# Where the modulation sums are accumulated, and where relu's squares stand before they are split

## The chip, the cores and the metric

The kernel runs on one core of one Trainium2 chip. The metric is device time in microseconds (us); before the change it is 3557.34 us, the median of 3 runs (3553.0 to 3562.2).

## What is computed

Two transformer blocks run one after the other on 512 tokens of 1024 features, all in fp32. The first block has two layers (a sparse and a stick-breaking attention side by side, then a feed-forward part). The second has two layers as well (latent attention, then a gated linear attention); it also sees 256 context tokens, and its norms are scaled and shifted by a modulation that is computed from one vector `c`, and for the context from `c_ctx`. Cut to what the change touches:

```python
# both blocks, each layer
ff = jnp.square(jax.nn.relu(hf @ w_ff1)) @ w_ff2        # [512, 1024] @ [1024, 4096], then back

# second block, each of two layers; ada_w[i] is [1024, 6144]
m_lat = (silu_c  @ ada_w[i] + ada_b[i]).reshape(B, N_MOD, 1, D)
m_ctx = (silu_cc @ ada_w[i] + ada_b[i]).reshape(N_MOD, D)
```

## The kernel before

TensorE (PE) does the large products on float32r operands. Every fp32 operand is kept as two float32r parts: `split` (lines 163 to 167) lets ScalarE (ACT) cast x to the high part and VectorE (DVE) subtract it from x for the low part; `wload` (169 to 195) does the same for a block of a weight with ACT and GpSimd (POOL, L194, two operations a block). `mac3` (208 to 213) then issues three products for one (L211, L212, L213). `feat_major` makes one tile, 128 features by up to 512 tokens, in one PSUM bank.

PSUM's eight banks are three pools: `mm` with two, `s` with four, `tp` with two. A tile's buffer is reused when the last instruction that reads it has ended. Weights in raw form have three buffers (`wraw`), their parts two each.

**The feed-forward part** (`mlp`, from line 619) goes through 8 chunks of 512 hidden features. `first(c + 1)` computes the 4 tiles of the next chunk, each of 24 products, in the two `mm` banks in turn (in chunk 0 in `mm` and `s` by turns, with 256 tokens at a time); then `second(c)` multiplies the chunk before with the second weight, 8 tiles of 12 products, in `mm` and `s` by turns. After each of the first product's tiles `square_parts` (517 to 530) takes relu's square from the bank and leaves its two parts in SBUF tiles `hid`: L522 on VectorE takes max(ps, 0) * r into an SBUF tile `t` (r is the norm's factor; in the second block there is none, and ACT takes the relu), L525 on ACT squares `t` into the high part of `hid`, L529 on VectorE squares `t` in place (in chunk 0 ACT does it, L527), and L530 subtracts.

**The modulation** (`ada`, from line 1334) is a vector times a matrix, made on VectorE as a background of the first block's two feed-forward parts: layer 0's modulation beside the first, layer 1's beside the second. For each of 12 groups u of 512 columns there are accumulators `aacc`, [128, 512] in SBUF, two of them (for `c` and for `c_ctx`; layer 1 needs the second only for the first four groups). Four steps q each load 512 KB of the matrix (`araw`, two buffers, one load ahead) and add two row blocks to each accumulator:

```python
nc.vector.scalar_tensor_tensor(a, raw[:, k], sc, a, op0=ALU.mult, op1=ALU.add)     # L1372
```

The first of a group writes without adding (L1370). Then `total` (1345 to 1355) splits each accumulator (L165 on ACT, L166 on VectorE, into SBUF tiles `t`), lets PE sum over the partitions with a column of ones, once for each part (L1351, L1352, into a `tp` bank), copies the row that results and sends it to DRAM. `total` of a group is called at the beginning of the next. When all groups are there, the sums are read back and transposed into the tiles `mod`.

**What sets the order.** `mlp` steps the background twice ahead of each weight block of the first product and three times (`BG`) ahead of `second`. The program is a stream of instructions in one order, and the tile framework's scheduler sorts it into the queues of the engines; each engine then works through its queue in order, and a product, or a VectorE operation, that has to wait holds up all that stands behind it on that engine. Loads are issued by SyncE (SP), in their own queue. The fp32 sums of the norms (`total` of line 276, L280) use plain fp32 operands and the ones tile `ones`; the sums of `ada` use `onesr`, its float32r form.

## Time and profile before

| | before |
|---|---|
| median of 3 runs | 3557.34 us |
| span of the profiled execution | 3557.3 us |
| busy: PE, DVE, ACT, POOL | 93%, 64%, 43%, 33% of the span |
| feed-forward parts of the first block | about 505 to 905 and 1445 to 1850 us |
| of the second block | about 2300 to 2770 (two streams) and 3200 to 3525 us |

The profiled execution is as long as the median run, so its microseconds can be set against the runs one to one. Instruction rows give the start in us, the duration, the engine, the line of the kernel and the tile written <- the tiles read; a wait in brackets is the engine's idle time ahead of it with what released it. PEclk is the clock that TensorE was granted, as a share of full speed.

### The profile page before, as it was taken

To read this page: it belongs to the slowest core of one execution; us is meant where nothing else is said; L and a number is where in the kernel's file an instruction comes from. 1 tells how busy PE (TensorE), PEld (TensorE's weight loads), DVE (VectorE), ACT (ScalarE), POOL (GpSimd) and SP (SyncE) were. 2 spreads that over 40 slices of the span, in tenths; PEclk is the share of its full clock that TensorE was granted. 3 is DMA by queue.
4 is the path that set the end of the run, shared out by engine and by line. 5 is a ranking of instruction groups with operands and counts; after the bars stand their busy time and mean duration, and the time that the engine had idled before them with its cause. 6 is when DMAs were issued, how large, how long until landed. Compare 5 with 4: busy or idle time off the path is not lost.

```text
span 3557.3 us, 49004 instructions
## 1 busy us (share of the span) xinstructions
PE 3299.7 (93%) x18723; PEld 2843.9 (80%) x18723; DVE 2263.8 (64%) x4044; ACT 1516.0 (43%) x3323; POOL 1191.2 (33%) x688
## 2 busy tenths in 40 slices
PE   8899988988989998989999999999999899889998
PEld 8788776766878887767778888888888788878887
DVE  6755668887686567886657763723433866873445
ACT  5455543222454454432235654531221456654223
POOL 3333334333333324334431332132232222124443
PEclk8999999999999999999999999999999999999999
DMA  5212444444232235345321113122122212123332
GB/s 171 66 60 75 166 140 152 135 145 131 82 92 72 74 114 177 116 158 176 119 74 59 37 60 97 48 63 68 60 64 63 69 53 66 63 70 95 95 95 77
DMA packets 262097, 337.68 MB, mean 95 GB/s; under 512 B 17107, under 2 KB 178110, under 8 KB 261734
## 3 DMA queue, kind: packets, MB, share of 16 engines
q1 hardware_dynamic: 261862, 334.55, 29.9%
q8 instruction: 147, 2.41, 0.3%
q14 instruction: 88, 0.72, 0.1%
HBM read 305.98 MB, written 28.52 MB: 94 GB/s over the span
## 4 chain that ended last, share of the span: by engine, by line
PE 62%; DVE 22%; ACT 8%; issue 5%; DMA 2%; POOL 1%; SPq 0%; DVEq 0%; ACTq 0%; POOLq 0%
PE mm L211 13%; PE mm L213 13%; PE mm L212 13%; PE s L212 4%; PE s L211 4%; PE s L213 4%; DVE aacc L1372 3%; ACT wh L190 2%; PE s L280 2%; DMA araw<-in_ada_w_dram 2%; DVE t L166 1%; PE tp L1065 1%; DVE t L529 1%; DVE wl L194 1%; PE mm L238 1%
## 5 line engine op out<-in xcount | busy, mean ns | idle before, releaser
L194 POOL TENSOR_TENSOR wl<-wraw,wh 128x1024 fp32r<-128x1024 f32 (+2 forms) x424 | 1008.4, 2397 | 1848.4 <-ACT wh L190 1800.2
L211 PE MATMUL mm<-h,wh 128*128 128x512 f32 (+1 forms) x1916 | 728.4, 380 | 30.1 <-ACT h L1264 8.5
L213 PE MATMUL mm<-h,wh 128*128 128x512 f32 (+1 forms) x1916 | 713.6, 373 | 6.0 <-DVE h L333 3.0
L212 PE MATMUL mm<-h,wl 128*128 128x512 f32 (+1 forms) x1916 | 716.4, 374 | 2.0 <-POOL wl L194 1.6
L190 ACT CAST wh<-wraw 128x1024 fp32r<-128x1024 f32 (+3 forms) x454 | 428.4, 967 | 512.1 <-issue 328.7
L211 PEld LDWEIGHTS mm<-h,wh 128*128 128x128 f32 x1916 | 370.2, 193 | 93.1 <-ACT h L1264 10.3
L213 PEld LDWEIGHTS mm<-h,wh 128*128 128x128 f32 x1916 | 369.1, 193 | 71.6 <-DVE h L1265 4.8
L212 PEld LDWEIGHTS mm<-h,wl 128*128 128x128 f32 x1916 | 371.0, 194 | 54.8 <-POOL wl L194 2.4
L529 DVE TENSOR_TENSOR t<-t 128x512 f32<-128x512 f32 (+1 forms) x140 | 169.2, 1208 | 256.3 <-ACT hid L525 256.0
L1372 DVE SCALAR_TENSOR_TENSOR aacc<-araw,sc,aacc 128x512 f32<-128x512 f32 x280 | 295.3, 1079 | 43.8 <-DMA araw<-in_ada_w_dram 41.8
L211 PE MATMUL mm<-hid,wh 128*128 128x512 f32 (+1 forms) x848 | 294.2, 347 | 9.7 <-DVE y L541 9.7
L212 PE MATMUL mm<-hid,wl 128*128 128x512 f32 (+1 forms) x848 | 292.4, 345 | 0.0
L213 PE MATMUL mm<-hid,wh 128*128 128x512 f32 (+1 forms) x848 | 291.3, 344 | 0.0
L541 DVE TENSOR_TENSOR y<-y,mm 128x512 f32<-128x512 f32 (+1 forms) x192 | 105.4, 549 | 201.7 <-PE mm L213 201.5
L211 PE MATMUL s<-hid,wh 128*128 128x512 f32 (+1 forms) x560 | 211.5, 378 | 0.0
L213 PE MATMUL s<-hid,wh 128*128 128x512 f32 (+1 forms) x560 | 211.4, 377 | 0.0
L212 PE MATMUL s<-hid,wl 128*128 128x512 f32 (+1 forms) x560 | 211.2, 377 | 0.0
L530 DVE TENSOR_TENSOR hid<-t,hid 128x512 fp32r<-128x512 f32 (+1 forms) x176 | 180.5, 1029 | 29.8 <-ACT t L527 25.4
L525 ACT ACTIVATE hid<-t 128x512 fp32r<-128x512 f32 (+1 forms) x176 | 97.2, 554 | 231.3 <-DVE t L522 155.6
L211 PEld LDWEIGHTS mm<-hid,wh 128*128 128x128 f32 x848 | 160.7, 190 | 33.0 <-DVE y L541 6.8
L213 PEld LDWEIGHTS mm<-hid,wh 128*128 128x128 f32 x848 | 160.7, 190 | 21.2
L212 PEld LDWEIGHTS mm<-hid,wl 128*128 128x128 f32 x848 | 160.7, 190 | 21.1 <-issue 0.3
(682 smaller groups left out, 7438.1 us busy)
## 6 DMA issues: line engine op xcount, KB each, us to landing
wraw<-in_w_ff_dram SPq DMA_DIRECT2D x128, 512.0 KB
wraw<-in_mlp_w_dram SPq DMA_DIRECT2D x128, 512.0 KB
araw<-in_ada_w_dram SPq DMA_DIRECT2D x96, 512.0 KB
wraw<-in_w_in_dram SPq DMA_DIRECT2D x68, 512.0 KB
raw<-in_cmp_w_dram SPq DMA_DIRECT2D x16, 512.0 KB
td<-t SPq DMA_DIRECT2D x32, 256.0 KB
h<-td SPq DMA_DIRECT2D x32, 256.0 KB
wraw<-in_w_out_dram SPq DMA_DIRECT2D x16, 512.0 KB
```

Of the source, the lines that this page charges most:

```text
L166: self.nc.vector.tensor_tensor(l, x, h.bitcast(F32), op=ALU.subtract)
L190: i = nc.scalar.copy(h[:, x:z], raw[:, x - a:z - a]).ins
L194: e.tensor_tensor(l[:, x:z], raw[:, x - a:z - a], h[:, x:z].bitcast(F32), op=ALU.subtract)
L211: nc.tensor.matmul(ps, wh, mh, start=first, stop=False)
L212: nc.tensor.matmul(ps, wl, mh, start=False, stop=False)
L213: nc.tensor.matmul(ps, wh, ml, start=False, stop=last)
L280: self.nc.tensor.matmul(ps, self.ones, acc, start=first, stop=last)
L525: nc.scalar.activation(h, a, AF.Square)
L529: nc.vector.tensor_tensor(a, a, a, op=ALU.mult)
L530: nc.vector.tensor_tensor(lo, a, h.bitcast(F32), op=ALU.subtract)
L541: nc.vector.tensor_tensor(y, y, ps, op=ALU.add)
L1372: nc.vector.scalar_tensor_tensor(a, raw[:, k], sc, a, op0=ALU.mult, op1=ALU.add)
```

## The change

In `ada`, the accumulators are no longer SBUF tiles but the two banks of `tp`. A new `part` splits them when the group's last step is issued, into SBUF tiles `ada0` and `ada1` of float32r; where layer 1 has two accumulators, ACT only copies them to fp32 tiles instead. `total` then has the ones-products and the row's copy alone, with its result in a bank of `s`. It is called after the third step of the next group, half a group later than before, and for copies in fp32 it is one product with `ones` instead of two with `onesr`. One more step is put ahead of the last `total`.

In `square_parts`, where one stream runs alone (the two feed-forward parts of the first block and the last one of the second), the square goes back into the bank that the product came from: with r ACT squares `t` into the bank, without r VectorE multiplies max(ps, 0) with ACT's relu into it. `split` then makes the two parts from the bank. The stage with two streams keeps what it had. In `load_ctx` the transposes of the context go to `s` instead of `tp`. Comments are dropped, too; the changed kernel's lines stand up to 20 lower in the file from `square_parts` on (L1370, L1372 are L1387, L1389 there; L1351 and L1352 are L1371).

```diff
-    def square_parts(self, ps, r, h, lo, quick):
+    def square_parts(self, ps, r, h, lo, bank, quick):
...
-        nc.scalar.activation(h, a, AF.Square)
-        if quick:
-            nc.scalar.activation(a, a, AF.Square)
+        if not bank:
+            nc.scalar.activation(h, a, AF.Square)
+            if quick:
+                nc.scalar.activation(a, a, AF.Square)
+            else:
+                nc.vector.tensor_tensor(a, a, a, op=ALU.mult)
+            nc.vector.tensor_tensor(lo, a, h.bitcast(F32), op=ALU.subtract)
+            return
+        if r is not None:
+            nc.scalar.activation(ps, a, AF.Square)
         else:
-            nc.vector.tensor_tensor(a, a, a, op=ALU.mult)
-        nc.vector.tensor_tensor(lo, a, h.bitcast(F32), op=ALU.subtract)
+            nc.vector.scalar_tensor_tensor(ps, ps, 0.0, a, op0=ALU.max, op1=ALU.mult)
+        self.split(ps, h, lo)
...
-            self.square_parts(ps, None if S.r is None else S.r[:, sl], h[:, sl], lo[:, sl], c == 0)
+            self.square_parts(ps, None if S.r is None else S.r[:, sl], h[:, sl], lo[:, sl], len(streams) == 1,
+                              c == 0)
...
-        def total(u, acc):
-            for s, a in enumerate(acc):
-                h = self.t(self.tmp, [P, 512], F32R, tag="t")
-                lo = self.t(self.tmp, [P, 512], F32R, tag="t")
-                self.split(a, h, lo)
-                ps = self.ps(pool=self.tp, tag="tp")
-                nc.tensor.matmul(ps[0:1], self.onesr[:, 0:1], h, start=True, stop=False)
-                nc.tensor.matmul(ps[0:1], self.onesr[:, 0:1], lo, start=False, stop=True)
+        def part(acc):
+
+            nb = 2 if l == 0 else 1
+            if l and len(acc) == 2:
+                out = [[self.t(pool, [P, 512], F32, tag=f"ada{q}", bufs=nb)] for q in range(2)]
+                for a, (c,) in zip(acc, out):
+                    nc.scalar.copy(c, a)
+                return out
+            out = [[self.t(pool, [P, 512], F32R, tag=f"ada{q}", bufs=nb) for q in range(2)] for _ in acc]
+            for a, hl in zip(acc, out):
+                self.split(a, *hl)
+            return out
+
+        def total(u, parts):
+            for s, ms in enumerate(parts):
+                ps = self.ps(pool=self.sp, tag="s")
+                one = (self.ones if len(ms) == 1 else self.onesr)[:, 0:1]
+                for q, m in enumerate(ms):
+                    nc.tensor.matmul(ps[0:1], one, m, start=q == 0, stop=q == len(ms) - 1)
...
-            if done:
-                total(*done)
-            acc = [self.t(pool, [P, 512], F32, tag="aacc", bufs=2) for _ in range(1 if l == 1 and u >= 4 else 2)]
+            acc = [self.ps(pool=self.tp, tag="tp") for _ in range(1 if l == 1 and u >= 4 else 2)]
...
+                if q == 2 and done:
+                    total(*done)
                 yield
-            done = u, acc
+            done = u, part(acc)
+        yield
         total(*done)
...
-                ps = self.ps(pool=self.tp, tag="tp")
+                ps = self.ps(pool=self.sp, tag="s")
```

**What moves.** PE, the sum of an early group in the first feed-forward part: of before, where a tile of the first product (`mm`, from the norm's parts `h` and the weight's parts `wh`, `wl`) has the two ones-products between its own.

```order
L213 MATMUL mm_6005<-h_4549,wh_5995 128x512
L211 MATMUL mm_6005<-h_4578,wh_5995 128x512
L212 MATMUL mm_6005<-h_4578,wl_5996 128x512
L213 MATMUL mm_6005<-h_4579,wh_5995 128x512
L1351 MATMUL tp_5981<-t_5977,onesr_642 1x512
L211 MATMUL mm_6005<-h_4608,wh_5995 128x512
L212 MATMUL mm_6005<-h_4608,wl_5996 128x512
L1352 MATMUL tp_5981<-t_5978,onesr_642 1x512
L213 MATMUL mm_6005<-h_4609,wh_5995 128x512
L211 MATMUL mm_6005<-h_4638,wh_5995 128x512
```

The changed kernel, where the sum of that group stands, between two tiles:

```order
L212 MATMUL mm_6023<-h_4740,wl_5984 128x512
L213 MATMUL mm_6023<-h_4741,wh_5983 128x512
L1371 MATMUL s_6065<-ada_1120_5967,onesr_642 1x512
L1371 MATMUL s_6065<-ada_1121_5968,onesr_642 1x512
L1371 MATMUL s_6071<-ada_1122_5969,onesr_642 1x512
L1371 MATMUL s_6071<-ada_1123_5970,onesr_642 1x512
L211 MATMUL mm_6087<-h_4548,wh_6077 128x512
L212 MATMUL mm_6087<-h_4548,wl_6078 128x512
L213 MATMUL mm_6087<-h_4549,wh_6077 128x512
```

The ones-products now come in one piece, four for the two accumulators, behind the last product of a tile and ahead of the next tile's first; before, the products of one accumulator stood apart, with two products of a tile between them.

VectorE, the square of a tile of the first product in the same part, and the sum's steps around it; of before:

```order
L522 SCALAR_TENSOR_TENSOR t_6508<-mm_6483,r_94 128x512
L1372 SCALAR_TENSOR_TENSOR aacc_6429<-araw_6437,sc_718,aacc_6429 128x512
L1372 SCALAR_TENSOR_TENSOR aacc_6430<-araw_6437,sc_718,aacc_6430 128x512
L1372 SCALAR_TENSOR_TENSOR aacc_6429<-araw_6513,sc_718,aacc_6429 128x512
L529 TENSOR_TENSOR t_6508<-t_6508 128x512
L1372 SCALAR_TENSOR_TENSOR aacc_6429<-araw_6513,sc_718,aacc_6429 128x512
L530 TENSOR_TENSOR hid_1185_6326<-t_6508,hid_1184_6325 128x512
L1372 SCALAR_TENSOR_TENSOR aacc_6430<-araw_6513,sc_718,aacc_6430 128x512
L166 TENSOR_TENSOR t_6526<-aacc_6429,t_6525 128x512
```

The changed kernel, at a tile of the same chunk (`mm_6379` and `mm_6441` are two tiles' banks, `tp_6417` and `tp_6418` the accumulators):

```order
L522 SCALAR_TENSOR_TENSOR t_6404<-mm_6379,r_94 128x512
L1389 SCALAR_TENSOR_TENSOR tp_6417<-araw_6425,sc_718,tp_6417 128x512
L1389 SCALAR_TENSOR_TENSOR tp_6418<-araw_6425,sc_718,tp_6418 128x512
L1389 SCALAR_TENSOR_TENSOR tp_6417<-araw_6501,sc_718,tp_6417 128x512
L166 TENSOR_TENSOR hid_1177_6310<-mm_6379,hid_1176_6309 128x512
L1389 SCALAR_TENSOR_TENSOR tp_6417<-araw_6501,sc_718,tp_6417 128x512
L1389 SCALAR_TENSOR_TENSOR tp_6418<-araw_6501,sc_718,tp_6418 128x512
L522 SCALAR_TENSOR_TENSOR t_6466<-mm_6441,r_94 128x512
L1389 SCALAR_TENSOR_TENSOR tp_6418<-araw_6501,sc_718,tp_6418 128x512
L166 TENSOR_TENSOR hid_1179_6312<-mm_6441,hid_1178_6311 128x512
```

The square's first step L522 is followed by the subtraction L166 that reads the same bank, with one to three steps of the sum between them, the last of which needs the next load (`araw_6501` behind `araw_6425`) at the first tile. L529 and L530, which work on SBUF tiles, are gone, and L166 reads the bank.

VectorE, the beginning of the feed-forward part, where the norm of the first tokens is closed (L260 and what follows); of before:

```order
L1372 SCALAR_TENSOR_TENSOR aacc_5209<-araw_5236,sc_718,aacc_5209 128x512
L1372 SCALAR_TENSOR_TENSOR aacc_5208<-araw_5236,sc_718,aacc_5208 128x512
L1372 SCALAR_TENSOR_TENSOR aacc_5209<-araw_5236,sc_718,aacc_5209 128x512
L299 TENSOR_TENSOR acc_95<-acc_95,t_4944 128x256
L299 TENSOR_TENSOR acc_95<-acc_95,t_4973 128x256
L299 TENSOR_TENSOR acc_95<-acc_95,t_5002 128x256
L299 TENSOR_TENSOR acc_95<-acc_95,t_5031 128x256
L260 TENSOR_SCALAR acc_95<-s_5093 128x256
L194 TENSOR_TENSOR wl_5223<-wraw_5224,wh_5222 128x512
```

The changed kernel:

```order
L299 TENSOR_TENSOR acc_95<-acc_95,t_5031 128x256
L1389 SCALAR_TENSOR_TENSOR tp_5604<-araw_5605,sc_718,tp_5604 128x512
L1389 SCALAR_TENSOR_TENSOR tp_5603<-araw_5611,sc_718,tp_5603 128x512
L1389 SCALAR_TENSOR_TENSOR tp_5604<-araw_5611,sc_718,tp_5604 128x512
L1389 SCALAR_TENSOR_TENSOR tp_5603<-araw_5611,sc_718,tp_5603 128x512
L1389 SCALAR_TENSOR_TENSOR tp_5604<-araw_5611,sc_718,tp_5604 128x512
L1389 SCALAR_TENSOR_TENSOR tp_5603<-araw_5687,sc_718,tp_5603 128x512
L1389 SCALAR_TENSOR_TENSOR tp_5604<-araw_5687,sc_718,tp_5604 128x512
L260 TENSOR_SCALAR acc_95<-s_5093 128x256
L1389 SCALAR_TENSOR_TENSOR tp_5603<-araw_5687,sc_718,tp_5603 128x512
L287 TENSOR_TENSOR ry_5098<-ry_5092 128x256
```

Between the last addition to `acc` (L299) and L260 stand now seven steps of the sum's second group (`tp_5603`, `tp_5604`), four of them from the load `araw_5611` and two from `araw_5687`; before there were none, and the last step ahead of them belonged to the first group (`aacc_5209`).

## Rows read from the trace of the kernel before

**Rows 1.** Page: busy time by engine; group of lines L190 (busy, mean ns).
```profile
PE 3299.7 (93%) x18723; PEld 2843.9 (80%) x18723; DVE 2263.8 (64%) x4044; ACT 1516.0 (43%) x3323; POOL 1191.2 (33%) x688
...
L190 ACT CAST wh<-wraw 128x1024 fp32r<-128x1024 f32 (+3 forms) x454 | 428.4, 967 | 512.1 <-issue 328.7
```

**Rows 2.** Windows: us; busy PE, PEld, DVE, ACT, POOL (instructions); PEclk, DMA share, GB/s.
```profile
505.00:905.00 400.00, 352.78 (x1540) 278.61 (x1541) 329.29 (x397) 118.57 (x181) 145.84 (x56) 0.95 0.42 131
1445.00:1850.00 405.00, 366.65 (x1625) 292.55 (x1624) 277.59 (x320) 116.93 (x175) 154.28 (x60) 0.96 0.43 136
3200.00:3525.00 325.00, 324.05 (x1465) 266.26 (x1463) 129.99 (x120) 101.73 (x142) 149.64 (x60) 1.00 0.30 93
```

**Rows 3.** Waits of PE, 505 to 905 us: total us, times, longest us.
```profile
PE tp L1352 <- DVE t L166: 38.7, 13, 6.3
PE tp L1351 <- ACT t L165: 5.5, 4, 3.6
```

**Rows 4.** Waits of PE, 1445 to 1850 us.
```profile
PE tp L1352 <- DVE t L166: 27.4, 11, 3.6
PE mm L211 <- DVE t L522: 5.0, 2, 2.5
PE tp L1351 <- ACT t L165: 4.8, 3, 3.2
```

**Rows 5.** Timeline of PE at 588 us: start, duration, instruction, idle before.
```profile
587.81 0.40 PE L212 MATMUL mm<-h,wl 128*128 128x512 f32 x1
594.51 0.58 PE L1352 MATMUL tp<-t,onesr 128*1 128x512 f32 x1 [6.30 <-DVE t L166]
```

**Rows 6.** Timeline of VectorE at the same place.
```profile
588.21 3.50 DVE L1372 SCALAR_TENSOR_TENSOR aacc<-araw,sc,aacc 128x512 f32<-128x512 f32 x2 [2.44 <-DMA araw<-in_ada_w_dram]
591.63 2.82 DVE L166 TENSOR_TENSOR t<-aacc,t 128x512 fp32r<-128x512 f32 x1
```

**Rows 7.** Timeline of GpSimd at the same place.
```profile
588.30 5.60 POOL L194 TENSOR_TENSOR wl<-wraw,wh 128x1024 fp32r<-128x1024 f32 x2 [6.49 <-ACT wh L190]
```

**Rows 8.** Lines L1372 and L522: ns min/median/max, first and last start.
```profile
L1372 DVE SCALAR_TENSOR_TENSOR aacc<-araw,sc,aacc x280: 736/747/2907, 456.0 to 1740.8; 128x512 f32<-128x512 f32 x140
...
L522 DVE SCALAR_TENSOR_TENSOR t<-mm,r x64: 409/684/693, 512.9 to 1810.6; 128x512 f32<-128x512 f32 x56, 128x256 f32<-128x256 f32 x8
```

**Rows 9.** Groups of VectorE, 505 to 905 us: count, busy us, mean ns, idle before.
```profile
L1372 DVE SCALAR_TENSOR_TENSOR aacc<-araw,sc,aacc 128x512 f32<-128x512 f32 x154 | 161.8, 1077 | 13.9 <-DMA araw<-in_ada_w_dram 13.1
L166 DVE TENSOR_TENSOR t<-aacc,t 128x512 fp32r<-128x512 f32 x24 | 33.7, 1404 | 4.5 <-ACT t L165 4.4
L529 DVE TENSOR_TENSOR t<-t 128x512 f32<-128x512 f32 x28 | 32.3, 1153 | 12.9 <-ACT hid L525 12.7
```

**Rows 10.** Windows of 14 us around two waits, columns as in rows 2.
```profile
587.00:601.00 14.00, 7.70 (x30) 5.69 (x29) 9.64 (x8) 3.21 (x5) 5.60 (x2) 0.76 0.43 144
658.00:672.00 14.00, 10.35 (x40) 7.80 (x41) 13.27 (x16) 3.16 (x5) 4.07 (x2) 0.88 0.41 122
```

**Rows 11.** Groups by form, whole span: the square, a cast and a subtraction from PSUM.
```profile
L525 ACT ACTIVATE hid<-t 128x512 fp32r<-128x512 f32 x112 | 70.9, 633 | 215.9 <-DVE t L522 147.8 <-PE s L212 66.7
L165 ACT CAST th<-tp 128x512 fp32r<-128x512 f32 x80 | 46.6, 589 | 52.6 <-PE tp L1065 52.0
...
L166 DVE TENSOR_TENSOR tl<-tp,th 128x512 fp32r<-128x512 f32 x80 | 54.7, 689 | 48.9 <-ACT th L165 48.3
```

**Rows 12.** Chain that ended last, 1520 to 1610 us: start, share of loads.
```profile
1580.57 4.30 DMA araw<-in_ada_w_dram
...
1600.71 7.45 DMA araw<-in_ada_w_dram
```

**Rows 13.** Timeline of VectorE ahead of the first feed-forward part.
```profile
468.67 10.70 DVE L1372 SCALAR_TENSOR_TENSOR aacc<-araw,sc,aacc 128x512 f32<-128x512 f32 x8 [8.62 <-DMA araw<-in_ada_w_dram]
```

**Rows 14.** Timeline of PE at a norm's plain fp32 ones-product.
```profile
511.99 0.59 PE L280 MATMUL s<-y,ones 128*128 128x256 f32 x2
...
512.53 0.28 PE L212 MATMUL s<-h,wl 128*128 128x256 f32 x1
```

## The prediction

> **What bounds the kernel now.** I read the page first: TensorE is busy 93% of the span [rows 1], so time can only come from where it stands still or runs slowly. The windows view then compares three feed-forward stages [rows 2]. The stage at 3200 to 3525 us has no modulation beside it: PE busy 324.05 of 325 us, granted clock 1.00. The two stages with the modulation sums beside the products (505 to 905 and 1445 to 1850) have PE busy 352.78 of 400 and 366.65 of 405, at clock 0.95 and 0.96. The waits of PE in these two stretches name the cause: the second ones-product (L1352) waits for the VectorE subtraction of `split` (L166) 38.7 us in 13 places and 27.4 us in 11, the first (L1351) for the ACT cast 5.5 and 4.8 us [rows 3, 4]. Products that wait for the square's first step (L522) lose 5.0 us in the second.
>
> One such place shows how it comes. PE starts a product at 587.81 and then nothing until the ones-product at 594.51, whose row gives 6.30 us of waiting for L166 [rows 5]. VectorE is in `aacc` (two operations 3.50 us, after a wait of 2.44 us for the load of araw), then in the subtraction, 2.82 us [rows 6]; GpSimd runs its wl subtractions from 588.30 for 5.60 us [rows 7]. So the slow VectorE operations lie on top of GpSimd's. By line: `aacc` takes 736 ns at its fastest and 2907 at its slowest, while L522, which has one operand in PSUM, never exceeds 693 ns [rows 8]. The mean is 1077 ns for `aacc`, 1404 for the sums' subtraction, 1153 for the square L529 [rows 9]: all three have both tensors in SBUF.
>
> **The change part by part.** *Sums.* The accumulators move into the two `tp` banks, each group is split as soon as it is complete, and the ones-products stand between two tiles' products half a group later, as the order shows on PE. A product at full clock takes 324.05 / 1465 = 0.221 us [rows 2], a tile of 24 takes 5.3. By the order the splits come out at least two tiles of products ahead of the ones-products, 10.6 us, against 6.3 us for the longest wait of today [rows 3]. Removed: 38.7 + 5.5 + 27.4 + 4.8 = 76.4 us [rows 3, 4]. What could come late next there is araw itself, which now delays only VectorE.
>
> *Clock.* A wait is followed by a lower granted clock, half speed for a while: 0.76 over the 14 us around the wait of 6.30 us, which is 0.24 x 14 = 3.4 us lost, and 0.88 around 658, 1.7 us lost [rows 10]. Over the stages the loss is 0.05 x 400 = 20 and 0.04 x 405 = 16 us [rows 2]. Stepping through the stages I count eighteen low stretches of which these two are samples, sixteen right behind a wait for a sum and two behind a wait for a bank; 16 of 18 would be 32, and I take 30 of the 36 us as given back. Together 106 us.
>
> *VectorE.* In the first stage 154 `aacc` operations go from 1077 ns to what an operation with one operand in PSUM takes. No row has VectorE writing to PSUM; the nearest are L522 (0.69) below and the undisturbed `aacc` (0.75) above; I take 0.7. That frees 154 x 0.38 = 58 us, the 28 squares L529 another 32, the 24 subtractions 24 x 0.7 = 17: some 107 of the 329 us that VectorE is busy there [rows 2, 9]. None of it is on PE's path by itself; it shortens VectorE's queue, which the next term needs. The Trainium skill ("VectorE: DVE Perf Modes", section "Why PSUM operands drop a tier") says that a PSUM operand takes an fp32 operation to one element a cycle. By that the first operation of a group (L1370) would lose its faster form; it stands beside other VectorE work, so the sum would not change by it.
>
> *The square in the product's bank.* Today a bank is free after L522, 0.69 us. Now it is held for L522, ACT's square into the bank, ACT's cast, and VectorE's subtraction. ACT writing to PSUM is in no row; its square into SBUF takes 633 ns, a cast from PSUM 589, the subtraction from PSUM 689 [rows 11], so 0.69 + 0.63 + 0.59 + 0.69 = 2.6 us at the least. `mm` has two banks and a tile takes 5.3 us, so 2.7 us are left for queueing. What queues: on VectorE up to four `aacc` operations (2.8 us) and, between the square's two steps, an operation that waits for araw (the second order extract); on ACT a pair of weight casts, 0.97 us each [rows 1], which wait for the products that used the buffer. I walked the second pair of tiles of a chunk with a load of araw at 4.3 us: the first tile's bank is free 2.8 us early, the second's 0.8 us early. Two loads of one stretch take 4.30 and 7.45 us [rows 12]. The bounds are 0 (all hidden) and 28 pairs x 2.35 = 66 us (every pair meets the slowest load: 7.45 - 4.3 - 0.8); I take 28 x 0.4 = 11, nearer the fast end, because the ordinary load is the fast one.
>
> *The start of the stage.* The order shows the second group of the accumulation now ahead of the VectorE steps that open the norm (L260), and each needs a load of araw; such a load has held VectorE 8.62 us at that place [rows 13]. PE waits for that norm. Bounds 0 and 2 x 8.6 = 17 us; I take 2 x 3 = 6, since VectorE is also through its earlier `aacc` sooner.
>
> *The fp32 ones-products.* For the first four groups of the second layer eight products with a plain fp32 operand replace two fast ones each. A plain fp32 ones-product of 256 columns shows as two records that take 0.59 us together, a fast product of as many columns 0.28 [rows 14], 0.31 less; at 512 columns that is 0.6 us, and 8 x 0.6 = 5 us (0, since the second fast product goes, to 8).
>
> *Nothing.* The last layer's stage runs PE at full clock without a wait [rows 2]; its bank is now held for ACT's relu, VectorE, ACT, VectorE, some 2.6 us by the same rows, plus one weight cast, under 5.3. Without that cover it would cost like the bank term. In the first chunk (c = 0) the tiles alternate between `mm` and `s` and the hold is hidden. The stage with two streams keeps its code, and the transposes of `load_ctx` that go from `tp` to `s` find four banks there. The copy of a sum's row and its small DMA move along with the ones-products; on SP they stand ahead of weight loads, and they no longer wait for a stopped PE, so I count nothing.
>
> **Sum:** 3557.3 - 76.4 - 30 + 11 + 6 + 5 = 3473 us. The profiled execution's span, 3557.3 us, is the median of the runs, so the sum holds for both.
>
> **The rivals.** *The banks give part of it back.* Slow araw loads in front of the bank's last reader, every pair: 66 instead of 11 us, and half the pairs followed by a dip of 1.7 us, 24: 3473 + 55 + 24 = 3552. With half of it the time is 3473 + 40 = 3513, this rival's middle. For it: two products already wait on L522 today. Against it: the walk leaves 0.8 us. The Trainium skill ("PSUM — Partial Sum Buffer", section "Summary: rules for kernel authors") says to evacuate PSUM promptly, and this part of the change does the opposite.
>
> *Slower than before.* The same bank hold, for every tile: if ACT's weight casts and four `aacc` operations both fall between a tile's steps, the release comes at 2.6 + 2.0 + 2.8 + one slow load's surplus 3.1 = 10.5 us, 5.2 us late, on 56 tiles (seven chunks of four in two stages) 290 us, so about 3473 - 11 + 290 = 3752. The point from which it decides: the other terms leave a gain of 95 us, 95 / 56 = 1.7 us late per tile, a release 7.0 us after the tile's last product. Against it: the order never has both in one tile.
>
> *The sums still wait.* If the splits were late in their new place, say because ACT's cast of an accumulator stands behind a weight cast, PE would wait as now and time be 3557 + 6 + 5 = 3568 at most; within 0.3% or just over it. Against: the distance in the order.
>
> *More than forecast.* Bank waits of today vanish too (5.0 us [rows 4] and two dips of 1.7, 8 us) and the three costs are nothing: 3557 - 106 - 8 = 3443, about 3440.
>
> **How the numbers follow.** Forecast 0.70 (own range 3440 to 3500), banks give part back 0.16 (3500 to 3552), more than forecast 0.04 (below 3440), sums still wait 0.05, slower 0.05. What a measurement of this kernel can tell from no change is about 0.3%, 11 us. Faster: 0.70 + 0.16 + 0.04 = 0.90; the same 0.05; slower 0.05. The range takes the forecast's own and most of the first rival: 3440 to 3520.
>
> **What would show it.** Right: in the two stages PE's waits for the ones-products are gone from the list, granted clock 0.98 or more, stages some 40 to 55 us shorter; `tp` operations of VectorE near 0.7 us whether or not GpSimd runs; L529 gone there. Wrong: a new line of PE waiting for L166 into `hid` or for ACT ahead of an `mm` product, with a dip behind it; L260 of the stage's start waiting behind `tp` operations; any PE wait in the last layer's stage. The forecast fails if loads of araw set VectorE's pace.

## The result, and the profile after

The changed kernel takes 3449.91 us (median of 4 runs, 3446.78 to 3452.52) against 3559.35 before: a ratio of 0.9697, 95% interval 0.9684 to 0.9710. The prediction was 3473, in a range of 3440 to 3520. The profiled execution's span is 3445.1 us, 112.2 less than before.

Page of the changed kernel, busy time by engine (beside rows 1):

```profile
PE 3270.0 (95%) x18723; PEld 2827.5 (82%) x18723; DVE 2001.6 (58%) x3988; ACT 1537.4 (45%) x3371; POOL 1158.8 (34%) x688
```

To set stages side by side I cut each feed-forward part from the first to the last product that reads `hid`, which is the same work in both kernels. Windows view of before, the two parts beside the modulation (columns as in rows 2):

```profile
557.80:946.80 389.00, 342.12 (x1497) 271.07 (x1498) 308.48 (x362) 110.90 (x165) 147.89 (x63) 0.95 0.41 127
1482.10:1864.30 382.20, 345.06 (x1516) 275.38 (x1517) 261.51 (x306) 108.90 (x165) 146.08 (x61) 0.96 0.42 133
```

The same cuts of the changed kernel:

```profile
553.90:882.50 328.60, 325.15 (x1494) 263.73 (x1493) 202.86 (x323) 118.63 (x187) 136.58 (x63) 0.99 0.46 146
1416.50:1753.30 336.80, 331.30 (x1512) 266.37 (x1512) 171.55 (x262) 117.49 (x185) 136.11 (x61) 0.99 0.45 145
```

The last part, of before and then of the changed kernel:

```profile
3230.60:3547.60 317.00, 315.17 (x1472) 260.22 (x1471) 133.66 (x144) 96.91 (x139) 139.40 (x60) 1.00 0.28 85
```

```profile
3118.00:3435.00 317.00, 315.19 (x1473) 260.29 (x1472) 88.65 (x144) 95.91 (x139) 133.62 (x60) 1.00 0.27 85
```

The first part is 60.4 us shorter, the second 45.4, together 105.8; granted clock rose from 0.95 and 0.96 to 0.99. The last part takes 317.0 us in both kernels. Of the other 6.4 us of the 112.2, 5.2 lie ahead of the parts: the first `hid` product comes 3.9 us earlier in the first, and the stretch up to the second part is 1.3 us shorter. What follows the second part is 1.2 us shorter.

Waits of PE in the changed kernel, 505 to 883 and then 1386 to 1754 us (beside rows 3 and 4; L548 is the old L541):

```profile
PE mm L211 <- DVE y L548: 3.3, 2, 2.2
PE mm L211 <- ACT h L332: 0.8, 1, 0.8
```

```profile
PE mm L211 <- DVE hid L166: 2.3, 4, 1.1
PE s L280 <- ACT y L322: 2.0, 1, 2.0
PE mm L211 <- DVE y L548: 1.1, 1, 1.1
```

No ones-product (L1371) waits any more. Waits for the bank that holds a square (L166 into `hid`) are 2.3 us in four places of the second part, in place of the 5.0 us at L522 [rows 4].

Lines of the changed kernel (beside rows 8), count, ns min/median/max: the accumulation, its first operation, the old form of which was L1370, and ACT's square into the bank:

```profile
L1389 DVE SCALAR_TENSOR_TENSOR tp<-araw,sc,tp x280: 740/750/757, 455.1 to 1626.7; 128x512 f32<-128x512 f32 x140
...
L1387 DVE TENSOR_SCALAR tp<-araw,sc x40: 737/746/756, 453.7 to 1616.5; 128x512 f32<-128x512 f32 x40
...
L534 ACT ACTIVATE mm<-t x64: 368/602/604, 513.6 to 1700.5; 128x512 f32<-128x512 f32 x56, 128x256 f32<-128x256 f32 x8
```

The slow cases of `aacc`, up to 2907 ns [rows 8], are gone altogether: the longest of 280 is 757 ns, while GpSimd ran the same 63 operations as before in the first part (136.58 us busy against 147.89).

### The profile page after: what moved, and what is told of

Read it like the earlier page. It is cut to its first block, busy times and chain, and to the rows that moved or that the text cites. A ratio compares the mean times of both kernels' runs of the same rounds, so it can differ in the third digit from the quotient of the medians.

```text
span 3445.1 us, 48973 instructions
## 1 busy us (share of the span) xinstructions
PE 3270.0 (95%) x18723; PEld 2827.5 (82%) x18723; DVE 2001.6 (58%) x3988; ACT 1537.4 (45%) x3371; POOL 1158.8 (34%) x688
## 4 chain that ended last, share of the span: by engine, by line
PE 40%; DVE 9%; ACT 2%; issue 1%; DMA 0%; POOL 0%; DVEq 0%; ACTq 0%; POOLq 0%
PE mm L211 9%; PE mm L213 9%; PE mm L212 9%; PE s L211 3%; PE s L212 3%; PE s L213 3%; PE s L280 1%; DVE y L350 1%; PE mm L239 1%; PE mm L240 1%; PE mm L238 1%; DVE y L308 1%; PE tp L1789 0%; DVE ry L287 0%; ACT wh L190 0%
## 5 line engine op out<-in xcount | busy, mean ns | idle before, releaser
L194 POOL TENSOR_TENSOR wl<-wraw,wh 128x1024 fp32r<-128x1024 f32 (+2 forms) x424 | 977.8, 2325 | 1767.4 <-ACT wh L190 1721.4
L212 PE MATMUL mm<-h,wl 128*128 128x512 f32 (+1 forms) x1916 | 709.0, 370 | 0.5 <-DVE wl L194 0.4
L190 ACT CAST wh<-wraw 128x1024 fp32r<-128x1024 f32 (+3 forms) x454 | 429.1, 968 | 546.4 <-issue 370.6
L211 PEld LDWEIGHTS mm<-h,wh 128*128 128x128 f32 x1916 | 366.0, 191 | 96.8 <-ACT h L332 10.7
L213 PEld LDWEIGHTS mm<-h,wh 128*128 128x128 f32 x1916 | 365.8, 191 | 67.9 <-DVE h L1273 4.8
L1389 DVE SCALAR_TENSOR_TENSOR tp<-araw,sc,tp 128x512 f32<-128x512 f32 x280 | 198.8, 751 | 69.2 <-DMA araw<-in_ada_w_dram 67.4
L548 DVE TENSOR_TENSOR y<-y,mm 128x512 f32<-128x512 f32 (+1 forms) x192 | 105.7, 550 | 223.6 <-PE mm L213 223.1
L548 DVE TENSOR_TENSOR y<-y,s 128x512 f32<-128x512 f32 x120 | 75.8, 632 | 150.4 <-PE s L213 150.1
L524 ACT ACTIVATE t<-mm 128x512 f32<-128x512 f32 (+1 forms) x94 | 48.2, 512 | 253.2 <-PE mm L213 253.1
L238 PE MATMUL mm<-wh,h 128*128 128x256 f32 x480 | 141.6, 296 | 1.4 <-ACT h L332 0.5
```

The source lines that it names most:

```text
L190: i = nc.scalar.copy(h[:, x:z], raw[:, x - a:z - a]).ins
L194: e.tensor_tensor(l[:, x:z], raw[:, x - a:z - a], h[:, x:z].bitcast(F32), op=ALU.subtract)
L211: nc.tensor.matmul(ps, wh, mh, start=first, stop=False)
L212: nc.tensor.matmul(ps, wl, mh, start=False, stop=False)
L213: nc.tensor.matmul(ps, wh, ml, start=False, stop=last)
L238: nc.tensor.matmul(ps, h[:, sl], w[0][:, k, :n], start=k == 0, stop=False)
```

## The experiments

The forecast came true, but it rested on two things at once, and the runs were chosen to part them. The **place**: the ones-products stand half a group later on PE. The **operand**: with an accumulator in PSUM VectorE's operations are no longer slow beside GpSimd's. The squares in the bank are a third part.

**Each part of the change alone.** The modulation's part, with the squares as before (the edit is against the changed kernel):

```diff
-            self.square_parts(ps, None if S.r is None else S.r[:, sl], h[:, sl], lo[:, sl], len(streams) == 1,
+            self.square_parts(ps, None if S.r is None else S.r[:, sl], h[:, sl], lo[:, sl], False,
                               c == 0)
```

> The modulation's part of the change without the squares in the bank (all three single-stream feed-forward parts keep the square in SBUF). Theory A (the gain is the sums' alone, the bank part neither costs nor gives): 3440 to 3462 us, within 0.3% of the changed kernel's 3450; L529 is back at a mean over 1.0 us and nobody waits for it. Theory B (VectorE's squares, which GpSimd slows, must go as well): 3475 us or more, with PE waiting for products' banks. Theory C, from the prediction's term of 11 us for the bank: the time falls below the changed kernel's, to about 3439.

Measured: 3447.82 us, ratio 0.9687 (0.9672 to 0.9701), the two parts 328.5 and 334.1 us. Theory A: the whole gain is there without the bank. In the profiled executions the bank costs 0.1 us in the first part and 2.7 in the second, not the 11 that theory C took over from the prediction; the medians of the two runs are not apart (ratios 0.9687 and 0.9697).

The squares in the bank alone (`square_parts` of the changed kernel put into the kernel before):

> The squares in the bank without the modulation's part: accumulators in SBUF, ones-products at the old place. Eleven waits of the kernel before last 3.65 us and hold a slow square L529 (2.46 us) ahead of the sums' subtraction; that square goes. Theory A: those eleven fall to about 1.2 us and lose their dips of the clock (1.7 us each), 11 x (2.4 + 1.7) = 45 us, so about 3515 us, and the sums still wait over 30 us in all. Theory B (the squares were the cause): 3470 us or less. Rival: nothing changes, since the subtraction alone still runs into GpSimd: 3550 us.

Measured: 3548.61 us, ratio 0.9972 (0.9962 to 0.9982). PE's waits in this run, 500 to 900 us (L1360 is the old L1352):

```profile
PE tp L1360 <- DVE t L166: 30.9, 19, 6.0
PE mm L211 <- DVE hid L166: 19.9, 6, 4.9
```

The time is near the rival's, the reason is not. The sums' waits did get shorter (31 us where rows 3 have 44), and in their place came 19.9 us for the banks: at each of the six places two `aacc` of 1.9 to 2.9 us stand in VectorE's queue ahead of the subtraction that frees the bank. The second part is 17 us shorter (365.4 us instead of 382.2), the first as long as before. So the prediction's rival that the banks give part back does exist, but only without the other half of the change.

**Operand or place.** Accumulators in PSUM, but `total` at its old place, at the beginning of the next group, with old squares (against the changed kernel):

```diff
         for u in range(12):
+            if done:
+                total(*done)
             acc = [self.ps(pool=self.tp, tag="tp") for _ in range(1 if l == 1 and u >= 4 else 2)]
...
-                if q == 2 and done:
-                    total(*done)
                 yield
             done = u, part(acc)
-        yield
         total(*done)
```

> Accumulators in PSUM, but the ones-products at the old place, at the beginning of the next group, and the squares in SBUF. If the operand decides (no slow operation, whatever the place): each sum waits only for a cast and a subtraction of 0.6 and 0.7 us, some 40 sums x 1 us, without dips: 3557 - 76 - 30 + 40 = 3491 us. If the place decides: PE still waits over 55 us, 3530 us or more, since the cast stands behind weight casts and the subtraction behind the square.

Measured: 3442.01 us, ratio 0.9673 (0.9657 to 0.9689). Windows view, the two parts:

```profile
552.50:880.70 328.20, 324.70 (x1494) 263.76 (x1493) 234.11 (x342) 106.07 (x162) 139.99 (x63) 0.99 0.46 143
1415.20:1748.40 333.20, 329.98 (x1513) 266.76 (x1513) 211.07 (x280) 104.78 (x160) 139.75 (x61) 0.99 0.45 143
```

It is as fast as with the late place, so the place isn't needed. It is also faster than either theory said. The trace has the reason: the splits have SBUF tiles of their own here (`ada0`, `ada1`) and are written as soon as VectorE has the last addition, 6.3 us at the least and 22.7 in the mean ahead of the ones-product that reads them (first part; end of L166 to start of the second product of each sum). In the kernel before that lead was 0.1 us at 13 of 24, since PE stood there until the subtraction ended.

The other half: late place and own tiles, but accumulators in SBUF. `part` and `total` of the changed kernel are put beside the old `total` in the kernel before, and used in the first part (l is 0) only; the second part and the squares keep the old code:

```diff
-            if done:
-                total(*done)
+            if done and l:
+                total_old(*done)
             acc = [self.t(pool, [P, 512], F32, tag="aacc", bufs=2) for _ in range(1 if l == 1 and u >= 4 else 2)]
...
+                if q == 2 and done and not l:
+                    total(*done)
                 yield
-            done = u, acc
...
+            done = u, acc if l else part(acc)
```

> The other half: accumulators stay in SBUF, but in the first feed-forward part (layer 0's modulation) they are split at the group's end and the ones-products come half a group later; the second part keeps the old code, and so do the squares. From the first to the last product of the second weight the first part took 389.0 us before and 328.6 in the changed kernel. If the place decides: 330 to 338 us there, in all about 3500 us. If the operand decides: over 350 us there, because slow subtractions and slow steps put VectorE behind, and PE waits for banks (L522) instead.

Measured: 3532.70 us, ratio 0.9931 (0.9916 to 0.9946). The first part, windows view, and PE's waits at 500 to 900 us:

```profile
560.20:926.10 365.90, 338.04 (x1495) 270.37 (x1495) 298.34 (x353) 106.74 (x162) 150.80 (x63) 0.96 0.42 132
```

```profile
PE mm L211 <- DVE t L522: 16.9, 8, 4.2
PE mm L211 <- DVE y L541: 6.1, 2, 5.6
PE mm L211 <- ACT h L332: 5.1, 3, 3.9
```

No ones-product waits, as in the changed kernel, and yet the part takes 365.9 us instead of 328.6. VectorE is nearly as busy as before (298.34 us against 308.48), and the waits move from the sums to the banks (L522, L541). The late place and the splits' own tiles alone bring 23 of the 60 us.

**The operand without any lead.** Three lines of the kernel before: accumulators in `tp`, the sums' results and the context's transposes in `s`; splits into the shared tiles `t`, place and squares as before.

```diff
-            acc = [self.t(pool, [P, 512], F32, tag="aacc", bufs=2) for _ in range(1 if l == 1 and u >= 4 else 2)]
+            acc = [self.ps(pool=self.tp, tag="tp") for _ in range(1 if l == 1 and u >= 4 else 2)]
...
-                ps = self.ps(pool=self.tp, tag="tp")
+                ps = self.ps(pool=self.sp, tag="s")
```

> The kernel before with three lines changed: the accumulators are the two tp banks, the sums' results and the context's transposes go to s. Splitting, its SBUF tiles from the shared ring, the place of the ones-products and the squares stay as they were, and no product is plain fp32. If the accumulator's place in PSUM is all that matters: 3442 (the run with the early sums) less eight plain fp32 products at 0.45 us more than two fast ones, so 3438 us, and PE's waits for the sums add up to under 8 us. If it was the parts' own tiles or the split in one piece that freed PE in that run: over 3470 us with waits at L1352.

Measured: 3485.33 us, ratio 0.9802 (0.9781 to 0.9824). That is over 3470 us with waits at L1352, so the accumulator's place in PSUM is not all that matters. What is left is in this timeline, VectorE and then GpSimd:

```profile
604.02 2.47 DVE L529 TENSOR_TENSOR t<-t 128x512 f32<-128x512 f32 x1 [0.97 <-ACT hid L525]
606.41 0.68 DVE L166 TENSOR_TENSOR t<-tp,t 128x512 fp32r<-128x512 f32 x1
607.01 2.27 DVE L530 TENSOR_TENSOR hid<-t,hid 128x512 fp32r<-128x512 f32 x1
609.20 0.74 DVE L1370 TENSOR_SCALAR tp<-araw,sc 128x512 f32<-128x512 f32 x1
```

```profile
603.53 5.19 POOL L194 TENSOR_TENSOR wl<-wraw,wh 128x1024 fp32r<-128x1024 f32 x2 [5.67 <-ACT wh L190]
```

This is the clearest row of the study. Within one pair of GpSimd operations, 603.5 to 608.7, VectorE's square with all tensors in SBUF takes 2.47 us, the subtraction from PSUM right behind it 0.68, and the next one on SBUF 2.27. The sum's subtraction is fast now, but it stands behind a slow square, and the ones-product stands right behind the subtraction: PE waits 20.0 and 11.1 us for L166 in the two parts, never over 1.8 at once, and 6.2 and 5.6 for the cast L165.

With the squares in the bank added, still without a lead:

> The run with three lines changed (3485 us) plus the squares in the bank: no sum has a slow operation of its own, none stands behind a slow square, but the ones-products still follow their splits at once. In the run without the bank 31 us of PE's waits at L1352 stood behind L529, 2.46 us on top of GpSimd. If those squares are what is left: the waits fall under 10 us, 3485 - 31 + 5 - some dips = 3435 to 3450 us. If the splits need the lead that their own tiles give them: 3470 us or more.

Measured: 3447.27 us, ratio 0.9686 (0.9672 to 0.9699), parts 337.0 and 335.6 us; waits for the sums add up to 3.1 us. So there are two cures for what the three lines leave: take the squares out of GpSimd's way too, or let the splits run ahead of the products, as in the early run. That run differs from the three lines in the splits' own tiles, in both accumulators being split in one piece, and in layer 1's fp32 copies; which of the first two gives the lead was not tried. The change has both cures, and one is enough.

**The cause itself.** GpSimd's part in the kernel before, beside the modulation, given to ACT, which copies the raw weight and leaves out the difference (`bg` is set while `mlp` has a background):

```diff
-                    e.tensor_tensor(l[:, x:z], raw[:, x - a:z - a], h[:, x:z].bitcast(F32), op=ALU.subtract)
+                    if e is nc.gpsimd and self.bg:
+                        nc.scalar.copy(l[:, x:z], raw[:, x - a:z - a])
+                    else:
+                        e.tensor_tensor(l[:, x:z], raw[:, x - a:z - a], h[:, x:z].bitcast(F32), op=ALU.subtract)
...
+        self.bg = bg is not None
```

> The kernel before, but beside the modulation (both feed-forward parts of the first block) the weight's low part is written by ACT as a copy of the raw weight and not by GpSimd as a difference, so the products there are not the reference's; ACT gets 64 more operations of about 1 us in each part. Theory (VectorE's operations with both tensors in SBUF are slow only on top of GpSimd's): aacc, L529 and L166 never exceed 0.8 us there; the sums' waits of 76 us fall to under 35, dips mostly gone, 3557 - 41 - 25 = about 3490 us, unless ACT's longer queue delays casts. Rival (they are slow for another reason, say the loads' traffic in SBUF): the maxima of 2.8 us stay.

Measured: 3428.32 us, ratio 0.9642 (0.9618 to 0.9667), parts 329.7 and 331.6. Accumulators, sums and squares are the old ones in SBUF, at the old place with the old tiles, and the whole gain is there and 20 us more. Most of the 20 lie ahead of the parts (the first `hid` product comes at 547.9 us, and 526.5 us lie between the parts), where the old order of the steps stands. I had taken only half of the waits to go.

The same with VectorE in GpSimd's place, which keeps the difference:

```diff
                     e = nc.vector if both and x == a else nc.gpsimd
+                    if self.bg:
+                        e = nc.vector
...
+        self.bg = bg is not None
```

> The kernel before, but in the first block's feed-forward parts VectorE makes the weights' low parts in GpSimd's place (L194, 64 operations of some 1.1 us more on VectorE a part, by 0.69 us for half as many columns); accumulators, squares and sums stay in SBUF at their old places. If GpSimd beside VectorE is the whole cause: 282 + 70 of some 385 us VectorE is busy, no operation above its undisturbed time, 3428 (GpSimd's work on ACT) to 3470 us. If a fuller VectorE queue makes the sums late anyway: 3500 us or more, with waits at L1352 and at products that wait for L194.

Measured: 3436.25 us, ratio 0.9656 (0.9643 to 0.9669), which is 15 us below the changed kernel's 3451.09 in its second measurement. Groups of VectorE in this run, 495 to 880 us (L1378 is L1372, L198 the weight's low part, L533 is L529, L168 is L166; beside rows 9):

```profile
L1378 DVE SCALAR_TENSOR_TENSOR aacc<-araw,sc,aacc 128x512 f32<-128x512 f32 x154 | 108.8, 746 | 2.9 <-DMA araw<-in_ada_w_dram 2.3
L198 DVE TENSOR_TENSOR wl<-wraw,wh 128x1024 fp32r<-128x1024 f32 x60 | 72.7, 1221 | 6.8 <-ACT wh L192 6.7
...
L533 DVE TENSOR_TENSOR t<-t 128x512 f32<-128x512 f32 x28 | 19.2, 688 | 3.7 <-ACT hid L529 3.5
...
L168 DVE TENSOR_TENSOR t<-aacc,t 128x512 fp32r<-128x512 f32 x24 | 16.5, 686 | 1.5 <-ACT t L167 1.5
```

With GpSimd busy for 6.9 of these 385 us the three means fall from 1077, 1404 and 1153 ns [rows 9] to 746, 686 and 688. VectorE takes on 60 operations of 1.22 us and gets back 53 + 17 + 13 us of its own: 161.8 - 108.8, 33.7 - 16.5, 32.3 - 19.2.

**What the bank can bear.** The changed kernel, with four more readings of each bank by ACT:

```diff
         self.split(ps, h, lo)
+        if r is not None and not quick:
+            for _ in range(4):
+                nc.scalar.copy(a, ps)
```

> The changed kernel with four further ACT copies that read the bank after its split, 4 x 0.58 = 2.3 us more hold of each bank of the first product (all chunks but the first, in the first block). By the prediction's walk the first tile of a pair has 2.8 us to spare and the second 0.8: 28 pairs x 1.5 = 42 us, half in each part, with dips up to 3515 us in all. If the hold has more room than that (a bank free 2.3 us early at every tile): no change, 3450 us.

Beside it, on the same chip, the changed kernel again:

> The changed kernel once more, beside the others on the same chip: 3450 us. If squares in the bank cost what the stages showed (336.8 us against 333.2 in the second part), it lies 3 to 12 us above the run with three lines changed; if the bank gives something, below it.

Measured: 3458.18 us with the longer hold, 3451.09 without, ratios 0.9726 (0.9701 to 0.9752) and 0.9705 (0.9683 to 0.9727), whose intervals overlap: 7 us between the medians, not clear of the noise. In the profiled executions the parts are 335.8 and 343.2 us against 328.6 and 336.8, 7.2 and 6.4 more, but the execution with the longer hold is the slowest of its four (3467.09). So 2.3 us more hold cost 14 us at the most, a third of the 42 by the walk. The changed kernel lies 34 us below the run with three lines, not 3 to 12 above it as expected, since that run was not as fast as the early one.

**In all stages.** L194 on VectorE everywhere, in the kernel before and in the changed one:

```diff
-                    e = nc.vector if both and x == a else nc.gpsimd
-                    e.tensor_tensor(l[:, x:z], raw[:, x - a:z - a], h[:, x:z].bitcast(F32), op=ALU.subtract)
+                    nc.vector.tensor_tensor(l[:, x:z], raw[:, x - a:z - a], h[:, x:z].bitcast(F32), op=ALU.subtract)
```

> The kernel before with every weight's low part made by VectorE (L194), in all stages and not only beside the modulation; 3436 us was the time with the two modulation stages alone. Elsewhere VectorE is busy 66% (0 to 440 us) and 67% (900 to 1400) of the time; 424 operations less 120 already moved, 304 x about 1.0 us, spread over 2800 us, take it to some 75%. If the place of the work decides everywhere as it does here: 3400 to 3430 us, since operations on SBUF lose their slow cases there, too. If the longer VectorE queue costs in stages whose chains run through it: 3440 to 3500 us.

Measured: 3319.40 us, ratio 0.9324 (0.9308 to 0.9339), more than expected. Page of this run:

```profile
PE 3230.9 (97%) x18723; PEld 2804.6 (84%) x18723; DVE 2204.7 (66%) x4484; ACT 1515.4 (46%) x3323; POOL 171.8 (5%) x248
```

> The changed kernel with every weight's low part made by VectorE, to be set beside the kernel before with the same edit (3319 us). If the change's whole gain is that it takes VectorE's operations out of GpSimd's way, it has nothing left to give here: 3315 to 3330 us, above 3319 by what it costs itself (the norm behind the sum's second group, some 4 us a stage; eight plain fp32 products, 4 us). If the place of the ones-products or the squares in the bank are worth something by themselves: under 3310 us.

Measured: 3317.79 us, ratio 0.9323 (0.9310 to 0.9336), 1.6 us below the kernel before with the same edit, whose ratio is 0.9324. Page:

```profile
PE 3231.2 (97%) x18723; PEld 2805.5 (85%) x18723; DVE 2179.3 (66%) x4428; ACT 1534.4 (46%) x3371; POOL 173.4 (5%) x248
```

Where GpSimd does not make the weights' low parts beside VectorE, the change is worth nothing that can be measured. Its whole gain of 109 us was the way out of GpSimd's way.

## Why the prediction was right, step by step

**The sum.** The forecast missed by 23 us (3473 against the median of 3450); in the profiled span, which can be cut by place, the change gave 112.2 us where the sum has 84, 28 more. Of these, 19 lie in the two parts. There 69.9 of the 76.4 us of waits were to go (the rest lies ahead of the cuts) and 30 of clock, less 11 for the bank and half of the 5 for fp32 products: 86 us, and 105.8 came. The bank took 3 us instead of 11 and the clock gave back 34. The waits for banks, which only the rival "more than forecast" let go, went as well, down to the 2.3 us at L166; in the kernel before, over the whole span, they were

```profile
PE mm L211 <- DVE t L522: 7.2, 3, 2.5
```

Another 7 of the 28 us lie at the stage starts, and 1 behind the second part.

**Sums: right in size, wrong in the reason.** The waits at L1351 and L1352 are gone, all 76.4 us of them [rows 3, 4]. The step said why: the ones-products stand half a group later, with two tiles of products, 10.6 us, between (in the first part of the changed kernel the splits are 7.5 us ahead at the least, 23.9 in the mean). The early run has the old place and the same time. In the late run with SBUF accumulators the sums do not wait either, but PE waits elsewhere, and 23 of 60 us are gained. It was the operand. The change moves both at once, so that the size held is luck as far as the place goes. What the prediction had as a side term, "none of it is on PE's path by itself", was the cause: slow operations of VectorE on top of GpSimd's. I had shown that in rows 6 to 9 and then priced the place. What holds of the step is that a lead helps where slow operations are left: the run with three lines needed 43 us more than the early run.

**Clock: right.** 0.95 and 0.96 became 0.99 over the cuts. Of 20 stretches at the lower level (1.2 GHz, a granted clock of 0.5) in the two parts, 75 us in all, 2 are left with 6.8 us: 34 us given back, where 30 of 36 were forecast.

**VectorE: right.** Its busy time in the first part fell by 106 us (308.48 to 202.86), as forecast (107). 0.7 us was taken for the operations with PSUM on one side; 0.75 (L1389) and 0.69 (L166 into `hid`) came. The first operation of a group went from a median of 479 to 746 ns, as the Trainium skill ("VectorE: DVE Perf Modes", section "Why PSUM operands drop a tier") let expect; the trace agrees, and nobody waits for it.

**The bank: 11 us forecast, 3 measured.** The chain was sized well: 0.69 + 0.60 + 0.58 + 0.69 = 2.56 us against 2.6, ACT's write to PSUM 602 ns against 633. The walk's slack of 0.8 us for the second tile of a pair was too small: four more readings, 2.3 us, should have cost 42 us and cost 14 at the most. Banks without the sums' cure do cost (19.9 us at the hand of slow `aacc`). To go against the rule of the Trainium skill to evacuate PSUM promptly ("PSUM — Partial Sum Buffer", section "Summary: rules for kernel authors"), which the prediction cited against this part, cost 3 us here.

**The start of the stage: the cost came, about as forecast, and was outweighed.** Two new waits of PE for the norm, in the changed kernel's timeline:

```profile
495.11 0.58 PE L211 MATMUL mm<-h,wh 128*128 128x256 f32 x1 [4.46 <-ACT h L332]
...
1355.55 0.38 PE L211 MATMUL mm<-h,wh 128*128 128x256 f32 x1 [3.93 <-ACT h L332]
```

That is 8.4 us, but in their place waits of the kernel before are gone: at each of the two starts (440 to 558 and 1380 to 1482 us) it has this line, which the changed kernel does not.

```profile
PE s L280 <- ACT y L322: 3.2, 2, 2.7
```

So the price of the order is better read from where the first `hid` products stand. In the run with three lines and in the one with the bank added, the second group's steps are not ahead of L260. There the first `hid` product comes at 550.8 and 552.0 us against 553.9, and the stretch up to the second part is 526.7 and 529.0 us against 534.0; 1.8 us of that difference are fp32 products. By the one run the order costs 3.1 + 7.3 - 1.8 = 9 us, by the other 5, around the 6 I took (single executions, and the stretch holds the attention, too). But a VectorE that GpSimd holds up less gains more at the same places: against 557.8 and 535.3 us of before, 15.6 us by the one run and 12.1 by the other, of which the sum had only the 6.5 us of waits for sums that lie there. So the stage starts came out 5 us shorter and not 6 longer.

**The fp32 products: 5 us forecast, about 4 measured.** Two of them, four records, and the product behind them in the changed kernel:

```profile
1456.21 1.88 PE L1371 MATMUL s<-ada,ones 128*1 128x512 f32 x4
1458.02 0.50 PE L211 MATMUL mm<-h,wh 128*128 128x512 f32 x1
```

Two products in 1458.02 - 1456.21 = 1.81 us are 0.9 each, against 0.45 for two float32r products (two steps of 0.22, [rows 2]): 8 x 0.45 = 3.6. Four of the eight stand ahead of the second part.

**The last layer: right.** 317.0 us before and after, and PE's waits there are the same, 1.8 us.

**The rivals.** The case of the banks giving back is real in the run with banks alone, not here. The sums did not still wait. Loads of araw did not set the pace: VectorE waits longer for them (82 us instead of 54), but PE hardly waits in the parts. Two of the signs of being wrong that the prediction lists did show, waits for L166 into `hid` (2.3 us) and L260 behind `tp` operations, and both were small. One rival was missing: that a smaller edit at the other engine gives more than the change.

## What to carry to other kernels

When an operation has two durations in the by-line view (736 and 2907 ns), find what runs beside the long cases before pricing a new order: here the cure was the partner, and moving GpSimd's subtraction to VectorE gave 3319 us where the change gave 3450. Work put on an idle engine is not free if it holds up a busy one; compare the busy time of both before and after. An order that gives producers a lead hides slow operations only up to the next queue that they delay.

## What the runs showed of the hardware

Operations of VectorE with two inputs in SBUF did not run side by side with GpSimd's subtractions. In the timeline above the second of VectorE's slow operations ends at 609.28, 0.56 us behind GpSimd's pair (608.72), and the one with a PSUM operand between the two is not touched. The same shows over the whole trace of the kernel before: of its 280 accumulations L1372, 51 take more than 0.8 us, and each of these ends 0.55 or 0.56 us behind a GpSimd operation; the 204 that meet none take 0.753 us at the most. The Trainium skill ("SBUF — State Buffer", section "SBUF: two separate sides") tells of such a shared pair of ports, locked for a whole instruction, for VectorE operations with two SBUF inputs against GpSimd ones that read SBUF; the traces agree. They also show that one input in PSUM is enough to be out of it: in the changed kernel 160 of the 280 accumulations meet a GpSimd operation, and none takes more than 757 ns.

I had not expected that VectorE would be no busier for doing GpSimd's work: with 440 more records it was busy 2204.7 us instead of 2263.8, because 1019 us of GpSimd went away. A 128x1024 subtraction took it 1221 ns beside the modulation, GpSimd 2535 in the mean before. What part of the 117 us between the two modulation stages (3436) and all stages (3319) comes from which place was not taken apart.
